# Twenty-four modulation columns of layer 0 computed as VectorE sums during the first mixer's output products, not as TensorE products during its projections

## The chip, the core and the metric

The kernel runs on one core of a Trainium2 chip. The metric is the time of one execution in microseconds (us). Three runs of the kernel before gave 1593.99, 1595.84 and 1599.15, so the median is 1595.84 us; the profiled execution, from which all durations below come, took 1600.35 us.

## What is computed

The reference is a trunk of two layers on a sequence of 512 tokens with 1024 features, all in float32. A conditioning vector `c` sets six vectors of 1024 numbers for each layer (shift, scale and gate of two sub-layers); these are the modulation:

```python
c_act = jax.nn.silu(c)
for l in range(DEPTH):                                   # DEPTH = 2
    mod = c_act @ w_ada[l] + b_ada[l]                    # 1024 x 6144
    sh_mix, sc_mix, gt_mix, sh_mlp, sc_mlp, gt_mlp = split(mod, 6)
    h = rms_norm(x, g_pre_mix[l]) * (1 + sc_mix) + sh_mix
    y = mixer(h, ...)       # w_in; 4 mLSTM heads; 8 groups of a causal depthwise conv (31 taps); w_out
    x = x + gt_mix * rms_norm(y, g_post_mix[l])
    h = rms_norm(x, g_pre_mlp[l]) * (1 + sc_mlp) + sh_mlp
    f = square(relu(h @ w_ff1[l])) @ w_ff2[l]
    x = x + gt_mlp * rms_norm(f, g_post_mlp[l])
```

## The kernel before

Features lie on the 128 partitions, so `x` is 8 tiles of 128x512, and the modulation of a layer is 48 columns of 128 numbers: columns 0 to 7 and 8 to 15 are shift and scale of the first norm, 16 to 23 the gate of the mixer, 24 to 39 shift and scale of the second norm, 40 to 47 the gate of the MLP.

A weight block of 128x1024 is loaded by SyncE's queue into one of four buffers `raw`, split by ScalarE into a rounded part (`whi`, L189) and by GpSimd into the rest (`wlo`, L190); the activations are split into such pairs too. Each product is then three passes on TensorE (L197 to L199). A `gemm` with one block is 24 passes of 128x512.

The mixer runs a list of steps (`ORDERS`, L66) by letter and number. `X` and `V` make the input and the short conv of an mLSTM head, `Q` its q, k, v and (L604) its part of the gate sums, `E` the gates from them (L614, L615), `G` one of the conv group's inputs, `Z` an output gate. `C` is the 31-tap conv of two groups on VectorE, 31 steps of 128x512 each (L450), with the group norm behind it (`conv_norm`: transposes L500 and L515 on TensorE, statistics L506 and L507, last product L521). `a` makes the weights of a head (products L683, on VectorE L675 and L685), `b` its output and norm (products L695, statistics L701 and L702, a power on GpSimd L165, scaling L715), `c` transposes it back (L724) and gates it (L726). `O` is one product with the conv half of `w_out`, whose eight input pairs are split by ScalarE and GpSimd (L173, L174). `finish` (L381) then runs the mLSTM half of `w_out`, adds (L397), and does the norms; it is the first to read columns 16 to 39.

The modulation is computed in two ways. `ada_rows` (L252) makes four columns on TensorE: four loads of 512 KB, eight products of 32x512 (L265), a copy on ScalarE (L268), four turning products (L270), and up to four small VectorE operations (L276, L278). `ada_col` (L282) makes one column on VectorE: one load of 512 KB into one of three buffers `adr`, and a product with the broadcast `c` that is summed along the row (L292, an instruction on 128x1024 and one that reads the sum out). Before the change, columns 0 to 15 of layer 0 are made ahead of the mixer by both ways, columns 16 to 39 by the six steps N4 to N9 of the first mixer's list, and the other 56 columns by `ada_col` in the first MLP. A new sum is put behind the instruction that `last[0]` names.

The program is written in this order, but a scheduler sets the order in which each engine issues; each engine then runs its instructions in that order, and a waiting instruction holds up all behind it. SyncE's queue is such an engine too: a load that waits for its buffer holds up the loads behind it.

Of the kernel before, what the change touches and what calls it, by code (L numbers as in the profile page):

```python
# [53 lines left out]
def trunk(ctx, tc, xT, vecs, bg, cst, ccol, crow, wadn, wadt, win, win0, wqkv, wgate, wout, wff1, wff2, yT):  # L54
    nc = tc.nc
    pe, dve, act, pool, sp = nc.tensor, nc.vector, nc.scalar, nc.gpsimd, nc.sync
# [6 lines left out]
    ps = ctx.enter_context(tc.tile_pool(name="ps", bufs=1, space=PSUM))  # L63

    NSLOT = 25
    ORDERS = ['X0 G3 V0 X1 Q0 V1 N4 G4 X2 G5 N5 Q1 V2 X3 N6 Q2 V3 G6 Q3 E G7 N7 Z0 Z1 Z2 Z3 N8 a0 Z4 b0 Z5 a1 b1 Z6 N9 c0 C0 a2 Z7 c1 b2 C1 C2 C3 O0 O1 a3 O2 c2 O6 O3 b3 O4 O5 c3 O7', 'X0 V0 G3 X1 Q0 V1 X2 G4 Q1 V2 G5 X3 Q2 V3 G7 Q3 E Z0 G6 Z1 Z2 Z3 a0 Z4 Z5 b0 a1 Z6 b1 Z7 c0 a2 c1 C0 b2 C1 C2 C3 O0 O1 a3 O6 O2 c2 O3 b3 O4 O5 c3 O7']  # L66
    WPRI = 300
    NK = 4
    KM = 4
# [182 lines left out]
    def ada_rows(nb, tag, alloc=None):  # L252


        bk = bank(tag)
        for kk in range(NF // 2):
            if alloc is not None:
                raw = alloc().rearrange("p a b -> p (a b)")
            else:
                raw = wpool.tile([P, D], F32, name="adr", tag="adr", bufs=ADR)  # L260
            load(raw, wadn[nb, kk])
            for j in range(2):
                k = 2 * kk + j
                g = k % 4
                pe.matmul(bk[32 * g:32 * g + 32, :], cc[:, k:k + 1].broadcast_to([P, 32]), raw[:, j * T:(j + 1) * T],  # L265
                          start=(k < 4), stop=(k >= 4), skip_group_check=True)
        rows = s2()
        act.copy(out=rows, in_=bk)  # L268
        for j in range(4):
            pe.matmul(bk[:, j:j + 1], rows[:, j * P:(j + 1) * P], cs[:, C_SEL:C_SEL + 1], start=True, stop=True)  # L270
        parts = [(2 * nb, 0, 2), (8 + 2 * nb, 2, 2)] if nb < 4 else [(4 * nb, 0, 4)]
        for c, o, n in parts:
            gain = ADA[c // 8][1]
            m, src = mods[0][:, c:c + n], bk[:, o:o + n]
            if gain is not None:
                dve.tensor_tensor(m, src, vec(gain, 0)[:, c % 8:c % 8 + n], op=ALU.mult)  # L276
                src = m
            dve.tensor_tensor(m, src, inits[0][:, c:c + n], op=ALU.add)  # L278

    late, last = [], [None]  # L280
# [155 lines left out]
    def mixer(l, hp, pre):  # L436
# [58 lines left out]
        def conv_norm(i, acc):  # L495
            csb = scr.tile([P, T], F32, name="csb", tag="csb", bufs=2)
            act.copy(out=csb, in_=acc)
            tp = bank("cx", (P, NC, P))
            for c in range(NC):
                pe.transpose(tp[:, c, :], csb[:, c * P:(c + 1) * P], ident)  # L500
            st = small(NC * 6, tag="cst6", bufs=2)
            mv = small(NC * 2, tag="cst2", bufs=2)
            stv = st.rearrange("p (c k) -> p c k", k=6)
            mvv = mv.rearrange("p (c k) -> p c k", k=2)
            for c in range(NC):
                dve.bn_stats(out=stv[:, c, :], in_=tp[:, c, :])  # L506
                dve.bn_aggr(out=mvv[:, c, :], in_=stv[:, c, :])  # L507
            r = rsqrt(mvv[:, :, 1], NC, "cm", eps=4.0 * EPS)
            ct = scr.tile([P, NC, P], F32, name="csb", tag="csb", bufs=2)
            for c in range(NC):  # L510
                dve.tensor_scalar(ct[:, c, :], tp[:, c, :], mvv[:, c, 0:1], r[:, c:c + 1],
                                  op0=ALU.subtract, op1=ALU.mult)
            bk = bank("cx")
            for c in range(NC):
                pe.transpose(bk[:, c * P:(c + 1) * P], ct[:, c, :], ident)  # L515
            th = scr.tile([P, T], F32, name="cth", tag="csb", bufs=2)
            act.activation(out=th, in_=bk, func=AF.Tanh, scale=hgb[:, l, i:i + 1], bias=hgb[:, l, 8 + i:9 + i])
            yv = cav(i)
            act.activation(out=bk, in_=bk, func=AF.Identity, scale=vec("g_cn", l)[:, i:i + 1],
                           bias=vec("b_cn", l)[:, i:i + 1])  # L520
            dve.scalar_tensor_tensor(yv, th, 1.0, bk, op0=ALU.add, op1=ALU.mult)  # L521

        def cav(i):
            if i // 2 not in caf:
# [220 lines left out]

        at[0], at[1], at[2] = glu_start(3)
        spare[0] = YM
        hm = []
        for step in ORDERS[l].split():
            i = int(step[1:] or 0)  # L750
            if step[0] == "X":
                do_xm(i)
            elif step[0] == "V":
                do_xc(i)
            elif step[0] == "G":
                at[i] = glu(i)
            elif step[0] == "Q":
                do_qkv(i)
            elif step[0] == "Z":
                z_proj(i)  # L760
            elif step[0] == "a":
                head_a(i, *g)
            elif step[0] == "b":
                head_b(i, *g)
            elif step[0] == "c":
                hm += head_c(i)
            elif step[0] == "C":
                accs = conv31([2 * i, 2 * i + 1])
                with tc.high_priority(offset=4000):
                    conv_norm(2 * i, accs[0])  # L770
                    conv_norm(2 * i + 1, accs[1])
                if i == 3:
                    ca = [conv_split(j) for j in range(NF)]
                    ypair = [slot() for _ in range(NF // 2)]
                    y = [ypair[j // 2][:, j % 2, :] for j in range(NF)]
            elif step[0] == "O":
                o = gemm([wout[l, 1, i]], ca)
                act.copy(out=y[i], in_=o)
            elif step[0] == "N":
                ada_rows(i, "ax")  # L780
            else:
                g = gates()
        return finish(l, "mix", [wout[l, 0, m] for m in range(NF)], hm, y, [ytile] * 2 + [slot] * KM,
                      ([wff1[l, m] for m in range(NK)], [slot] * NK))

# [99 lines left out]
def _layout(inp):  # L885
    f = lambda n: np.asarray(inp[n])
    col = lambda a: a.reshape(L, -1, P).transpose(2, 0, 1)
    parts = []
    for name, w in VEC_SPECS:
        a = f(name)  # L890
        if name in ("w_conv_m", "w_dw"):
            k = a.shape[1]
            parts.append(a.reshape(L, k, NF, P).transpose(3, 0, 2, 1).reshape(P, L, NF * k))
        else:
            parts.append(col(a))
    vecs = np.concatenate(parts, axis=2)
    wg = f("w_gates").reshape(L, 3, 2, P, H, 2 * H)
    wg = wg.transpose(0, 3, 4, 1, 2, 5).reshape(L, P, 24, 2 * H)
    gate = np.zeros((L, P, 24, 32), np.float32)
    gate[..., :2 * H] = wg  # L900
    kmaj = lambda a, nk, nm: a.reshape(L, nk, P, nm, P).transpose(0, 3, 2, 1, 4)
    qkv = np.stack([f("w_q"), f("w_k"), f("w_v")], axis=2)
    wo = f("w_out").reshape(L, 2, 8, P, NF, P).transpose(0, 1, 4, 3, 2, 5)
    w2 = f("w_ff2").reshape(L, 2, 2, 8, P, NF, P).transpose(0, 1, 5, 2, 4, 3, 6)
    first = [c for j in range(4) for c in (2 * j, 2 * j + 1, 8 + 2 * j, 9 + 2 * j)] + list(range(16, 40))
    return {
        "xT": f("x")[0].T.reshape(NF, P, T),
        "vecs": vecs,
        "bg": f("b_gates").reshape(L, 2, H).transpose(2, 0, 1).reshape(H, 2 * L),
        "cst": const_array(),  # L910
        "ccol": f("c").reshape(NF, P).T,
        "crow": f("c").reshape(1, D),
        "wadn": f("w_ada")[0].reshape(D, 48, P)[:, first].reshape(4, 2, P, 10, T).transpose(3, 0, 2, 1, 4).reshape(10, 4, P, D),
        "wadt": f("w_ada").transpose(0, 2, 1).reshape(L, 48, P, D),
        "win": kmaj(f("w_in"), 8, 32).reshape(L, 32, P, 1024),
        "win0": kmaj(f("w_in"), 8, 32)[0, [24, 16, 25, 17, 26, 18]].reshape(6, P, 8, P).transpose(2, 1, 0, 3).reshape(NF, P, 6 * P),
        "wqkv": qkv.reshape(L, H, 3, 2, P, DH).transpose(0, 1, 2, 4, 3, 5).reshape(L, H, 3, P, 512),
        "wgate": gate,
        "wout": wo.reshape(L, 2, NF, P, 1024),
        "wff1": kmaj(f("w_ff1"), 8, 32).reshape(L, 32, P, 1024),  # L920
        "wff2": w2.reshape(L, 2, NF, 2, P, 1024),
    }
# [18 lines left out]
```

## Time and profile before

| What | Value |
|---|---|
| Median of three runs | 1595.84 us |
| Profiled execution, span within it | 1600.35 us, 1598.6 us |
| TensorE matmuls | 1541.6 us, 96% of the span |
| VectorE | 876.3 us, 55% |
| ScalarE, GpSimd | 690.3 us (43%), 799.3 us (50%) |
| DMA | 35.4% of the engines' time, 118 GB/s |
| Mean granted TensorE clock | 0.986 |

The shares are means over the span. The first mixer, on which the change bears, ends its list at about 401 us, where `finish` begins. In the timeline an entry gives its start and its length; several equal instructions in a row are one entry with a count, and a bracket gives the idle time before it and what ended that.

### The profile page before, as it was taken

The numbers are of one execution on the slowest core, as the hardware profiler recorded it, in microseconds if no ns is written. First come the engines' busy times: TensorE is split into PE (matmuls) and PEld (weight loads), VectorE is DVE, ScalarE is ACT, GpSimd is POOL, SyncE is SP. The second block draws the span as 40 slices with busy tenths as digits, with TensorE's granted clock in tenths as the row PEclk, the third lists the DMA queues.
The fourth block names the chain that finished last, engine by engine and source line by source line (L and its number), as shares of the span: only waits on it lengthen the run. The fifth ranks groups of instructions, "written<-read, shape, count | busy, mean of one in ns | idle before, by whom it ended". The sixth has DMA issues, their size and how long they took to land.

```text
span 1598.6 us, 21226 instructions
## 1 busy us (share of the span) xinstructions
PE 1541.6 (96%) x8020; PEld 1258.7 (79%) x8020; DVE 876.3 (55%) x1761; ACT 690.3 (43%) x1168; POOL 799.3 (50%) x488
## 2 busy tenths in 40 slices
PE   5999999999999999999999999999999999999997
PEld 4776756678998888888899777676799888888887
DVE  6799998742363521347667999997226320012114
ACT  3364653444554322332463656545355432233242
POOL 0275743256744444445772877426564444444462
PEclk9999999999999999999999999998999999999999
DMA  8524323303423555556630222220241233223241
GB/s 318 188 80 147 130 96 127 137 27 106 135 64 119 185 198 180 191 192 237 214 113 1 80 74 89 82 67 27 93 146 53 85 101 93 92 92 94 97 126 54
DMA packets 56270, 188.91 MB, mean 118 GB/s; under 512 B 6376, under 2 KB 8552, under 8 KB 56168
## 3 DMA queue, kind: packets, MB, share of 16 engines
q1 hardware_dynamic: 56168, 187.56, 35.4%
q8 instruction: 63, 1.03, 0.3%
q14 instruction: 39, 0.32, 0.1%
HBM read 185.44 MB, written 2.10 MB: 117 GB/s over the span
## 4 chain that ended last, share of the span: by engine, by line
PE 78%; DVE 3%; ACT 2%; POOL 1%; issue 0%; DMA 0%; POOLq 0%; ACTq 0%
PE ps_mm L197 23%; PE ps_mm L199 23%; PE ps_mm L198 23%; PE ps_mm L695 2%; PE ps_mm L683 2%; PE ps_ax L337 1%; POOL wlo L190 1%; ACT whi L189 1%; PE ps_ax L265 1%; PE ps_ax L670 0%; PE ps_ax L599 0%; PE ps_ax L363 0%; DVE ps_cv L450 0%; PE ps_ax L724 0%; PE ps_cx L500 0%
## 5 line engine op out<-in xcount | busy, mean ns | idle before, releaser
L190 POOL TENSOR_TENSOR wlo<-raw,whi 128x1024 fp32r<-128x1024 f32 (+1 forms) x216 | 498.5, 2309 | 541.7 <-ACT whi L189 522.2
L197 PE MATMUL ps_mm<-slot,whi 128*128 128x512 f32 (+1 forms) x1632 | 621.8, 382 | 6.8 <-ACT slot L173 3.4
L199 PE MATMUL ps_mm<-slot,wlo 128*128 128x512 f32 (+1 forms) x1632 | 622.7, 382 | 4.7 <-POOL wlo L190 4.7
L198 PE MATMUL ps_mm<-slot,whi 128*128 128x512 f32 (+1 forms) x1632 | 621.2, 381 | 0.0
L189 ACT CAST whi<-raw 128x1024 fp32r<-128x1024 f32 (+1 forms) x216 | 216.4, 1002 | 509.9 <-PE ps_mm L198 369.7
L197 PEld LDWEIGHTS ps_mm<-slot,whi 128*128 128x128 f32 x1632 | 307.5, 188 | 74.8 <-issue 4.4
L199 PEld LDWEIGHTS ps_mm<-slot,wlo 128*128 128x128 f32 x1632 | 307.6, 188 | 71.3 <-POOL wlo L190 7.1
L198 PEld LDWEIGHTS ps_mm<-slot,whi 128*128 128x128 f32 x1632 | 307.6, 188 | 67.3 <-issue 5.5
L450 DVE SCALAR_TENSOR_TENSOR ps_cv<-slot,vv,ps_cv 128x512 f32<-128x512 f32 x480 | 332.6, 748 | 1.5
L790 DVE TENSOR_TENSOR ps_mm<-rl,ps_mm 128x512 f32<-128x512 f32 (+1 forms) x78 | 46.8, 600 | 282.5 <-ACT rl L789 282.4
L197 PE MATMUL ps_mm<-slot 128*128 128x256 f32 (+1 forms) x568 | 159.7, 293 | 9.6 <-DVE slot L792 7.4
L198 PE MATMUL ps_mm<-slot 128*128 128x256 f32 (+1 forms) x568 | 163.3, 292 | 0.2
L199 PE MATMUL ps_mm<-slot 128*128 128x256 f32 (+1 forms) x568 | 161.8, 289 | 0.0
L197 PEld LDWEIGHTS ps_mm<-slot 128*128 128x128 f32 x568 | 106.6, 192 | 13.0 <-DVE slot L792 8.2
L198 PEld LDWEIGHTS ps_mm<-slot 128*128 128x128 f32 x568 | 109.0, 192 | 3.2 <-issue 0.8
L199 PEld LDWEIGHTS ps_mm<-slot 128*128 128x128 f32 x568 | 108.8, 192 | 1.3
L190 POOL TENSOR_TENSOR slot<-raw,slot 128x1024 fp32r<-128x1024 f32 x34 | 86.4, 2563 | 12.8 <-issue 11.2
L165 POOL TENSOR_TENSOR small<-small,mhalf 128x4 f32<-128x4 f32 (+1 forms) x38 | 34.2, 900 | 95.5 <-DVE small L164 90.7
L292 DVE CUSTOM_DVE_ANT_0 adr<-adr,cbc,ini 128x1024 f32<-128x1024 f32 x40 | 65.4, 1645 | 23.2 <-DMA adr<-in_wadt 23.1
L792 DVE TENSOR_TENSOR slot<-ps_mm,slot 128x512 fp32r<-128x512 f32 (+1 forms) x78 | 46.4, 595 | 38.2 <-ACT slot L791 38.0
L551 POOL TENSOR_TENSOR xa<-xa,s 128x512 f32<-128x512 f32 x48 | 62.0, 1291 | 5.1 <-ACT xa L546 1.8
L791 ACT CAST slot<-ps_mm 128x512 fp32r<-128x512 f32 (+1 forms) x78 | 39.9, 511 | 46.0 <-DVE ps_mm L790 46.0
(204 smaller groups left out, 1577.3 us busy)
## 6 DMA issues: line engine op xcount, KB each, us to landing
raw<-in_wff SPq DMA_DIRECT2D x138, 512.0 KB, 3.5
raw<-in_win SPq DMA_DIRECT2D x58, 512.0 KB, 3.3
adr<-in_wadt SPq DMA_DIRECT2D x56, 512.0 KB, 4.5
raw<-in_wout SPq DMA_DIRECT2D x36, 512.0 KB, 3.5
adr<-in_wadn SPq DMA_DIRECT2D x28, 512.0 KB, 4.1
raw<-in_wqkv SPq DMA_DIRECT2D x24, 256.0 KB, 2.6
slot<-in_wadt SPq DMA_DIRECT2D x8, 512.0 KB, 8.6
raw<-in_win SPq DMA_DIRECT2D x8, 384.0 KB, 7.2
```

The costliest lines, as they stand in the source:

```text
L165: pool.tensor_tensor(y, u, mhalf[:, 0:n], op=ALU.pow)
L189: act.copy(out=r32(hi), in_=raw)
L190: wlast[0] = (lo_eng or pool).tensor_tensor(r32(lo), raw, hi, op=ALU.subtract)
L197: pe.matmul(out, whi, xh, start=first, stop=False)
L198: pe.matmul(out, whi, xl, start=False, stop=False)
L199: mark[0] = pe.matmul(out, wlo, xh, start=False, stop=last)
L292: red = dve.tensor_tensor_reduce(raw, raw, cbc, scale, 0.0 if one else ini, ALU.mult, ALU.add, m)
L450: dve.scalar_tensor_tensor(acc, at[i][:, k:k + T], w, acc, op0=ALU.mult, op1=ALU.add)
L551: pool.tensor_tensor(acc, acc, tk, op=ALU.add)
L790: dve.tensor_tensor(o, rl[:, ts], o, op=ALU.mult)
L791: act.copy(out=r32(pr[:, 0, ts]), in_=o)
L792: last[0] = dve.tensor_tensor(r32(pr[:, 1, ts]), o, pr[:, 0, ts], op=ALU.subtract)
```

## The change

The steps N4 to N9 leave the first mixer's list. In their place, from step C3 on, two `ada_col` calls follow each step until the columns 16 to 39 are done, and `ada_bias` adds the bias of the scales behind the list. `conv_norm` now names its last product (L521) in `last[0]`, so that no sum goes ahead of the latest group norm that is written before it. The `wadn` array loses the six blocks that N4 to N9 read.

```diff
-    ORDERS = ['X0 G3 V0 X1 Q0 V1 N4 G4 X2 G5 N5 Q1 V2 X3 N6 Q2 V3 G6 Q3 E G7 N7 Z0 Z1 Z2 Z3 N8 a0 Z4 b0 Z5 a1 b1 Z6 N9 c0 C0 a2 Z7 c1 b2 C1 C2 C3 O0 O1 a3 O2 c2 O6 O3 b3 O4 O5 c3 O7', ...
+    ORDERS = ['X0 G3 V0 X1 Q0 V1 G4 X2 G5 Q1 V2 X3 Q2 V3 G6 Q3 E G7 Z0 Z1 Z2 Z3 a0 Z4 b0 Z5 a1 b1 Z6 c0 C0 a2 Z7 c1 b2 C1 C2 C3 O0 O1 a3 O2 c2 O6 O3 b3 O4 O5 c3 O7', ...
@@ conv_norm
-            dve.scalar_tensor_tensor(yv, th, 1.0, bk, op0=ALU.add, op1=ALU.mult)
+            last[0] = dve.scalar_tensor_tensor(yv, th, 1.0, bk, op0=ALU.add, op1=ALU.mult)
@@ mixer
-        hm = []
+        hm, ahead = [], []
...
-            elif step[0] == "N":
-                ada_rows(i, "ax")
             else:
                 g = gates()
+            if l == 0 and step == "C3":
+                ahead = [(0, c) for c in range(16, 40)]
+            for _ in range(2):
+                if ahead:
+                    ada_col(*ahead.pop(0))
+        ada_bias()
```

Three places of the issue order show what the scheduler makes of it. Line numbers in the changed kernel are lower by one from L268 on. The first place is VectorE at the end of the last group norm. Before, head 1's statistics (L701, L702) and gating (L726) follow the norm's last product; in the changed order sums (L291, with `adr`) follow it, and between them stand operations that make head 2's weights (L684 and L674, the L685 and L675 of before; `s2` is such a weight tile). Before, behind the last L521:

```order
L521 SCALAR_TENSOR_TENSOR yt_2904<-cth_2938,ps_cx_2933 128x512
L701 BN_STATS small_2159<-slot_2140 128x6 x2
L702 BN_AGGR small_2160<-small_2159 128x2 x2
L701 BN_STATS small_2159<-slot_2140 128x6
L702 BN_AGGR small_2160<-small_2159 128x2
L726 TENSOR_TENSOR s2_2261<-ps_ax_2256,slot_1826 128x512
```

and now (the instruction that reads a sum out is left out behind each):

```order
L520 SCALAR_TENSOR_TENSOR yt_2756<-cth_2790,ps_cx_2785 128x512
L291 ISA adr_2822,mod0_101<-adr_2822,cbc_76,ini0_103,vv_74 128x1024
...
L291 ISA adr_2825,mod0_101<-adr_2825,cbc_76,ini0_103,vv_74 128x1024
...
L291 ISA adr_2860,mod0_101<-adr_2860,cbc_76,ini0_103,vv_74 128x1024
...
L684 SCALAR_TENSOR_TENSOR s2_2255<-ps_mm_2261,s2_2255 128x512
L674 SCALAR_TENSOR_TENSOR s2_2265<-ps_ax_2253,cols_1617,cs_73 128x128
L291 ISA adr_2863,mod0_101<-adr_2863,cbc_76,ini0_103,vv_74 128x1024
...
L291 ISA adr_2898,mod0_101<-adr_2898,cbc_76,ini0_103,vv_74 128x1024
```

The head's operations now stand behind and between sums; the first three sums have their data, and the fourth needs a buffer that the first frees.

The second place is VectorE at the end of head 2's norm (step b2), whose scaling (L714, before L715) TensorE's transposes of step c2 read; L712 (before L713) needs the power that GpSimd computes from L164's result. Before:

```order
L164 TENSOR_SCALAR small_2528<-small_2524 128x4
L675 SCALAR_TENSOR_TENSOR s2_3063<-ps_ax_3034,cols_1691,cs_73 128x128
L685 SCALAR_TENSOR_TENSOR s2_3036<-ps_mm_3042,s2_3036 128x512
L713 TENSOR_TENSOR small_2531<-small_2527,small_2522 128x4
L715 TENSOR_SCALAR slot_2490<-slot_2490,small_2510,small_2531 128x256 x4
```

and now:

```order
L164 TENSOR_SCALAR small_2380<-small_2376 128x4
L291 ISA adr_3209,mod0_101<-adr_3209,cbc_76,vv_74 128x1024
...
L291 ISA adr_3212,mod0_101<-adr_3212,cbc_76,vv_74 128x1024
...
L712 TENSOR_TENSOR small_2383<-small_2379,small_2374 128x4
L684 SCALAR_TENSOR_TENSOR s2_2916<-ps_mm_2921,s2_2916 128x384
L714 TENSOR_SCALAR slot_2342<-slot_2342,small_2362,small_2383 128x256 x4
L291 ISA adr_3235,mod0_101<-adr_3235,cbc_76,vv_74 128x1024
```

`adr_3212` holds the 22nd of the 24 sums, so 22 sums now stand ahead of the scaling.

The third place is SyncE's queue, where `raw_3049` holds the weights of step O3 and `raw_3140` those of O4:

```order
L127 DMA raw_3049<-in_wout 128x1024
L127 DMA adr_2863<-in_wadt 128x1024
L127 DMA adr_2898<-in_wadt 128x1024
L127 DMA adr_2901<-in_wadt 128x1024
...
L127 DMA adr_3042<-in_wadt 128x1024
L127 DMA adr_3045<-in_wadt 128x1024
L127 DMA raw_3140<-in_wout 128x1024
L127 DMA adr_3080<-in_wadt 128x1024
```

Eleven loads for sums, each of which waits for a buffer, stand between the two weight blocks; before, these two followed one another without a load between them.

## Rows read from the trace of the kernel before

**Rows 1.** The page: busy time of each engine, and of its 40 slices of 40 us VectorE's busy tenths and the granted TensorE clock in tenths.

```profile
PE 1541.6 (96%) x8020; PEld 1258.7 (79%) x8020; DVE 876.3 (55%) x1761; ACT 690.3 (43%) x1168; POOL 799.3 (50%) x488
DVE  6799998742363521347667999997226320012114
PEclk9999999999999999999999999998999999999999
```

**Rows 2.** Busy time by stretches of 40 us in the first mixer. Columns: the stretch, its length, then busy us and instructions of PE, PEld, DVE, ACT, POOL, granted clock, DMA share, GB/s.

```profile
120.00:160.00 40.00, 40.00 (x194) 27.11 (x193) 38.53 (x70) 16.04 (x25) 22.92 (x19) 1.00 0.44 148
160.00:200.00 40.00, 40.00 (x197) 28.51 (x196) 37.63 (x72) 27.66 (x47) 30.62 (x25) 1.00 0.38 129
200.00:240.00 40.00, 36.82 (x160) 23.31 (x159) 38.44 (x72) 22.11 (x37) 19.80 (x17) 0.91 0.29 95
240.00:280.00 40.00, 36.48 (x169) 25.51 (x168) 35.44 (x83) 13.98 (x19) 13.03 (x7) 0.96 0.37 129
280.00:320.00 40.00, 40.00 (x185) 25.84 (x183) 30.34 (x83) 19.41 (x43) 10.08 (x6) 1.00 0.36 135
```

**Rows 3.** TensorE's products of N4 to N9: the groups of the stretch 120 to 330 us (busy us, mean ns), and two entries of the timeline.

```profile
L265 PE MATMUL ps_ax<-adr,cc 128*32 128x512 f32 x96 | 19.6, 646 | 0.0
L270 PE MATMUL ps_ax<-cs,s 128*128 128x1 f32 x48 | 6.0, 242 | 0.0
...
140.32 1.06 PE L265 MATMUL ps_ax<-adr,cc 128*32 128x512 f32 x8
141.32 1.05 PE L270 MATMUL ps_ax<-cs,s 128*128 128x1 f32 x8
```

**Rows 4.** VectorE's timeline: 24 steps of the conv, the last head's gate sum, the last step of the conv, the last product of the last group norm, and the first addition of `finish`.

```profile
69.71 15.89 DVE L450 SCALAR_TENSOR_TENSOR ps_cv<-slot,vv,ps_cv 128x512 f32<-128x512 f32 x24
229.91 0.69 DVE L604 TENSOR_TENSOR gsb<-gsb,ps_ax 128x512 f32<-128x512 f32 x1 [0.56 <-PE ps_ax L599]
300.34 0.74 DVE L450 SCALAR_TENSOR_TENSOR ps_cv<-slot,vv,ps_cv 128x512 f32<-128x512 f32 x1
317.75 0.68 DVE L521 SCALAR_TENSOR_TENSOR yt<-cth,ps_cx 128x512 f32<-128x512 f32 x1
403.92 0.42 DVE L397 TENSOR_TENSOR slot<-slot,ps_mm 128x256 f32<-128x256 f32 x1 [7.57 <-PE ps_mm L199]
```

**Rows 5.** TensorE's timeline: the gates' first product, the last transposes of the last group norm, the transposes of step c2 and the products of head 3 behind them.

```profile
230.66 1.87 PE L614 MATMUL ps_mm<-gsb,cs 128*4 128x512 f32 x2 [0.78 <-DVE gsb L604]
315.06 0.60 PE L515 MATMUL ps_cx<-cs,csb 128*128 128x128 f32 x4
360.02 1.04 PE L724 MATMUL ps_ax<-cs,slot 128*128 128x128 f32 x8
360.89 1.47 PE L683 MATMUL ps_mm<-slot 128*128 128x256 f32 x8
```

**Rows 6.** VectorE's other operations of the stretch 80 to 345 us that step a, b and c use, by group (busy us, mean ns, idle before).

```profile
L685 DVE SCALAR_TENSOR_TENSOR s<-ps_mm,s 128x512 f32<-128x512 f32 (+3 forms) x12 | 5.8, 488 | 7.1 <-PE ps_mm L683 5.5 <-ACT s L679 1.3 <-ACT s L677 0.4
L675 DVE SCALAR_TENSOR_TENSOR s<-ps_ax,cols,cs 128x128 f32<-128x128 f32 x13 | 4.5, 347 | 5.0 <-PE ps_mm L695 3.3 <-ACT s L679 1.5 <-PE ps_ax L670 0.2
L701 DVE BATCH_NORM_STATS2 small<-slot 128x6 f32<-128x256 f32 x9 | 3.8, 425 | 1.9 <-ACT slot L697 1.8
L715 DVE TENSOR_SCALAR slot<-slot,small 128x256 f32<-128x256 f32 x8 | 2.9, 400 | 0.0
L726 DVE TENSOR_TENSOR s<-ps_ax,slot 128x512 f32<-128x512 f32 x4 | 2.8, 689 | 5.5 <-PE ps_ax L724 4.3 <-PE ps_mm L695 1.1
```

**Rows 7.** VectorE's timeline: sums of the first MLP (two that follow one another, the reading out of the second, and one later), and the same small operation of a head's norm at two times.

```profile
734.15 1.28 DVE L292 CUSTOM_DVE_ANT_0 adr<-adr,cbc,vv 128x1024 f32<-128x1024 f32 x1
735.35 3.43 DVE L292 CUSTOM_DVE_ANT_0 adr<-adr,cbc,vv 128x1024 f32<-128x1024 f32 x1
738.71 0.08 DVE L292 DVE_READ_ACCUMULATOR2_ANT mod<- 128x1 f32 x1
759.27 3.41 DVE L292 CUSTOM_DVE_ANT_0 adr<-adr,cbc,ini 128x1024 f32<-128x1024 f32 x1
...
325.57 0.16 DVE L710 TENSOR_TENSOR small<-small 128x4 f32<-128x4 f32 x1
351.05 1.19 DVE L710 TENSOR_TENSOR small<-small 128x4 f32<-128x4 f32 x1
```

**Rows 8.** GpSimd's timeline at the same times: weight splits, and the eight splits of the conv half.

```profile
734.48 3.22 POOL L190 TENSOR_TENSOR wlo<-raw,whi 128x1024 fp32r<-128x1024 f32 x1 [3.16 <-ACT whi L189]
755.85 2.40 POOL L190 TENSOR_TENSOR slot<-raw,slot 128x1024 fp32r<-128x1024 f32 x1 [1.35 <-ACT slot L189]
758.22 3.39 POOL L190 TENSOR_TENSOR wlo<-raw,whi 128x1024 fp32r<-128x1024 f32 x1
343.50 9.99 POOL L174 TENSOR_TENSOR slot<-yt,slot 128x512 fp32r<-128x512 f32 x8
```

**Rows 9.** The loads into `adr` in the stretch 730 to 785 us, where sums and weight loads follow one another fastest: from issue to landing.

```profile
DMA to landing us min/median/max: 3.2/3.8/5.2
```

**Rows 10.** Three stretches about an idle time of TensorE, with the columns of rows 2.

```profile
100.00:104.00 4.00, 1.74 (x8) 1.07 (x6) 4.00 (x7) 3.16 (x6) 3.07 (x3) 1.00 0.12 49
106.00:108.00 2.00, 2.00 (x6) 1.52 (x6) 2.00 (x4) 0.91 (x2) 2.00 (x3) 0.50 0.00 0
110.00:112.00 2.00, 2.00 (x7) 1.55 (x6) 2.00 (x4) 1.67 (x4) 1.68 (x2) 0.69 0.00 0
```

More of the change, by code (lines that the diff above doesn't have):

```diff
@@ L65, in trunk @@
     NSLOT = 25
-    ORDERS = ['X0 G3 V0 X1 Q0 V1 N4 G4 X2 G5 N5 Q1 V2 X3 N6 Q2 V3 G6 Q3 E G7 N7 Z0 Z1 Z2 Z3 N8 a0 Z4 b0 Z5 a1 b1 Z6 N9 c0 C0 a2 Z7 c1 b2 C1 C2 C3 O0 O1 a3 O2 c2 O6 O3 b3 O4 O5 c3 O7', 'X0 V0 G3 X1 Q0 V1 X2 G4 Q1 V2 G5 X3 Q2 V3 G7 Q3 E Z0 G6 Z1 Z2 Z3 a0 Z4 Z5 b0 a1 Z6 b1 Z7 c0 a2 c1 C0 b2 C1 C2 C3 O0 O1 a3 O6 O2 c2 O3 b3 O4 O5 c3 O7']
+    ORDERS = ['X0 G3 V0 X1 Q0 V1 G4 X2 G5 Q1 V2 X3 Q2 V3 G6 Q3 E G7 Z0 Z1 Z2 Z3 a0 Z4 b0 Z5 a1 b1 Z6 c0 C0 a2 Z7 c1 b2 C1 C2 C3 O0 O1 a3 O2 c2 O6 O3 b3 O4 O5 c3 O7', 'X0 V0 G3 X1 Q0 V1 X2 G4 Q1 V2 G5 X3 Q2 V3 G7 Q3 E Z0 G6 Z1 Z2 Z3 a0 Z4 Z5 b0 a1 Z6 b1 Z7 c0 a2 c1 C0 b2 C1 C2 C3 O0 O1 a3 O6 O2 c2 O3 b3 O4 O5 c3 O7']
     WPRI = 300
@@ L270, in ada_rows @@
             pe.matmul(bk[:, j:j + 1], rows[:, j * P:(j + 1) * P], cs[:, C_SEL:C_SEL + 1], start=True, stop=True)
-        parts = [(2 * nb, 0, 2), (8 + 2 * nb, 2, 2)] if nb < 4 else [(4 * nb, 0, 4)]
-        for c, o, n in parts:
+        for c, o, n in [(2 * nb, 0, 2), (8 + 2 * nb, 2, 2)]:
             gain = ADA[c // 8][1]
@@ L904, in _layout @@
     w2 = f("w_ff2").reshape(L, 2, 2, 8, P, NF, P).transpose(0, 1, 5, 2, 4, 3, 6)
-    first = [c for j in range(4) for c in (2 * j, 2 * j + 1, 8 + 2 * j, 9 + 2 * j)] + list(range(16, 40))
+    first = [c for j in range(4) for c in (2 * j, 2 * j + 1, 8 + 2 * j, 9 + 2 * j)]
     return {
@@ L912, in _layout @@
         "crow": f("c").reshape(1, D),
-        "wadn": f("w_ada")[0].reshape(D, 48, P)[:, first].reshape(4, 2, P, 10, T).transpose(3, 0, 2, 1, 4).reshape(10, 4, P, D),
+        "wadn": f("w_ada")[0].reshape(D, 48, P)[:, first].reshape(4, 2, P, 4, T).transpose(3, 0, 2, 1, 4).reshape(4, 4, P, D),
         "wadt": f("w_ada").transpose(0, 2, 1).reshape(L, 48, P, D),
```

## The prediction

> **What bounds the kernel now.** I read the page first, then the stretches of the first mixer, then timelines, for which engine's wait ends last in each stage. By the page TensorE works 96% of the span [rows 1], so any product taken from it looks like time won. But these products lie in one stage, and there the page's slices show VectorE at nine tenths. The stretches say it more sharply: from 120 to 280 us VectorE works 38.53, 37.63, 38.44 and 35.44 of each 40 us, idle 10 of 160, while TensorE has some idle time (36.82, 36.48) [rows 2]. So VectorE sets the pace up to the end of the conv at about 301 us [rows 4]; TensorE's products of the modulation are partly fill. From there to `finish` TensorE is full and VectorE's digits fall. I therefore ask when two things happen: when the last group norm's transposes run (T7, 315.06 before [rows 5]), and when TensorE gets through step c2's transposes (360.02 [rows 5]) to `finish`, whose first addition stands at 403.92 [rows 4]. Behind that the order of all engines is practically the same in both kernels, so the shift there is the shift of the end.
>
> **What is removed.** N4 to N9 hold 96 products (19.6 us busy) and 48 turning records (6.0) [rows 3]. Ends overlap: a group of eight takes about 1.05, so 12 + 6 groups are 18 to 19 us by starts, and 25.6 by busy time; with the waits on the copy between I take 24. The ten small VectorE operations and six ScalarE copies are little (about 1.4 us on VectorE before the last conv step). The 24 loads become 24 others of the same 512 KB; I cost them at nothing, since DMA is at 0.29 to 0.44 there [rows 2].
>
> **Step 1, the gates.** Head 4's gate sum stands at 229.91 and TensorE waits 0.78 for it [rows 4, 5]. In the changed order four conv steps of 0.66 (24 take 15.89 [rows 4]) and one L521 (0.68) stand behind it instead of ahead, and five modulation operations (0.8) are gone: 4.1 earlier, and 1.3 more as VectorE waits less for TensorE: 224.5. TensorE, without N4 to N6 (half of 24), would be there 12 earlier, at 218.7, so it waits 6 there: half of this gain goes.
>
> **Step 2, to the last conv step.** Before, 71.2 us lie from the gate sum's start to that step's end (300.34 + 0.74). Now the work of step 1 that moved behind and parts of heads 1 and 2 (three L675, four L685, statistics) come on top, by the durations in [rows 4, 6] about 7.3 net of removed operations. Some 7.5 of the 71.2 were idle; I take 5 of it back. 71.2 + 7.3 - 5 = 73.5, so the step ends at 298, not 301.
>
> **Step 3, T7.** From there to T7 were 14.0; with N9's turns out I take 13: T7 = 311. Bounds: 315 if the 14 us of TensorE work that now stand ahead of T7 (c0's transposes, Z6, a2's products) fill what was freed, 306 if step 2's idle goes altogether and step 1 loses nothing.
>
> **Step 4, VectorE from the last L521 to b2's scaling.** This is the step that decides. L521 ends 3.4 behind T7 (317.75 + 0.68 - 315.06 [rows 4, 5]). In the changed order 22 sums stand between it and b2's scaling, and step c2's transposes read what that scaling writes. TensorE runs in order, so c2 holds O2 and all behind. Its terms:
> - 22 sums of 1.28 and 0.08 for reading out [rows 7]: 29.9.
> - The others there: seven operations of a2, six of a3, two L726, four L701 with L702, about six small, four L715: by the means in [rows 6] about 11.
> - Waiting for data. With three buffers a sum can come every (3.8 + 1.36) / 3 = 1.72 us at the median landing and 2.19 at the longest [rows 9], against 1.86 of VectorE work per sum (40.9 / 22). Bounds 0 and 22 x 0.33 less what contention hides, at most 6.3; I take 2.
> - Contention with GpSimd. A sum beside a GpSimd split takes 3.43 and 3.41 instead of 1.28 [rows 7], and the split 3.22 and 3.39 instead of 2.40 [rows 8]. So the pair takes 3.4 where one after the other would take 3.68: only 0.28 is gained by overlap. Even a small operation went from 0.16 to 1.19 during the conv half's splits [rows 7, 8]. GpSimd has 17.3 us in this stretch: eight such splits (9.99 [rows 8]), two of the same length for the heads (2.5) and two weight splits (4.8). At 3.4 - 1.28 = 2.1 per 2.4, that is 15.5 at most, 0 if the splits fall beside other work or ahead; I take 10, nearer to the upper row, as the sums leave VectorE hardly a gap.
>
> 29.9 + 11 + 2 + 10 = 53, bounds 41 and 62.
>
> The Trainium skill has a rule that speaks against this change ("SBUF — State Buffer", section "Who interferes with whom"): a VectorE instruction with two SBUF inputs and a GpSimd instruction that reads SBUF shut each other out for whole instructions. By it each split would cost its full length, 17.3 for 15.5 at the upper end; the trace nearly agrees, 3.4 for the pair against 3.68.
>
> **Step 5, c2 to `finish`.** 403.92 - 360.02 = 43.9 before. Head 3's eight L683 (1.47 [rows 5]) now stand ahead of c2: 42.5. But TensorE's own work from T7 to c2 is only about 31 now (45 before less the 14 of step 3), against 56.4 of VectorE's chain, so it stands still for some 25 us. After an idle 2.26 of 4 us, about 102 us, the granted clock was 0.50 in one stretch and 0.69 in another some us later [rows 10]; so the first products behind a wait of 25 us may go at half speed too: 0 to 3 us, I take 1.7, about what those two stretches lost together (1.0 and 0.62 us).
>
> **Sum.** 311 + 3.4 + 53 + 42.5 + 1.7 = 411.6 for the first addition of `finish`, 7.7 later than 403.92. The profiled execution took 1600.35 us, 4.5 above the median of 1595.84; 1600.35 + 7.7 = 1608.1 stands to the median as 1604. The stretch of step 4 at which nothing changes is 53 - 7.7 = 45.
>
> **Rivals.**
> - **No change.** The stretch is 40.5 to 50 us, or T7 comes early: half of the contention taken (5 for 10) and no wait for data gives 46, and +1 us. For it: the eight splits of the conv half may run mainly before the first sums, since ScalarE writes their other half early. Against it: they stood at 343.50, 25 us behind the last L521 [rows 4, 8]. 1591 to 1601, middle 1596.
> - **The other side: VectorE hides the sums.** One mechanism: GpSimd's splits don't meet the sums, so that step 4 costs its own 41 us, and T7 comes early, at 306. Then c2 starts 17 earlier than in my forecast, without the wait that slows the clock, and `finish` at 306 + 3.4 + 41 + 42.5 = 392.9, 11 earlier: 1585. It decides from a stretch below 40.5 at T7 = 311, or 45 at 306. For it: VectorE has slack behind 320 us (30.34 of 40 in 280 to 320 [rows 2], four and two tenths of the slices after [rows 1]), and sums in the first MLP do run at 1.28 [rows 7]. The face value of the change, all 24 us, at 1572, is the far end of this; the bound of VectorE before 280 us speaks against it.
> - **SyncE's queue.** Eleven loads for sums stand ahead of O4's weight block. Each waits for a buffer, so that block is issued when the eleventh sum behind is through, about 28 us behind T7, and is split about 7 later; TensorE comes to O4 some 75 behind T7 (56.4 to c2, then O2, O6 and O3). It costs nothing unless sums are 40 us late; then those 40 would come on top of a kernel already slower, 1620 or more. It falls within slower.
> - **The change doesn't do what it says**: sums go elsewhere. The issue order shows them behind the last L521, so I give it nothing.
>
> **How the numbers follow.** A difference under 0.3%, 4.8 us, is about what a measurement of this kernel can't tell from none. Forecast, slower than that: the stretch is over 50 us, as three of its four terms have prices in the rows: 0.58, with 0.03 of SyncE's queue in it. No change: 0.26. The other side: 0.16, of which 0.03 for the face value. At the ends, 306 with 41 gives -11, 315 with 62 gives +22; both at once are unlikely, so the range is 1588 to 1614 (-8 and +18), which leaves out about one in ten on either side.
>
> **What would show it right or wrong.** Right: the last L521 at about 314.4; TensorE waiting some 6 us for the gate sum; sums of 2.3 to 3.4 us where GpSimd splits beside them and 1.28 elsewhere; b2's scaling done at about 367; an idle time of TensorE of 20 us or more ahead of c2's transposes, released by VectorE's scaling; a lower granted clock behind; the first addition of `finish` at about 411.6 and everything behind it as before. Wrong: c2 starts before 360, T7 before 306, or TensorE waits for a weight block of O4 or O5 rather than for VectorE.

## The result

The changed kernel takes 1615.42 us (median of four, 1614.96 to 1616.51) against 1597.49 of the kernel before (four runs beside it): slower, ratio 1.0117, 95% interval 1.0103 to 1.0131. The forecast was 1604, with a range up to 1614. The sign was right, and so was the mechanism in the first mixer. The loss is twice the forecast, mainly because as much again comes behind that mixer, where nothing was forecast.

The profiled execution took 1614.96 us. Against the profiled one of before that is 14.6 more: 7.5 up to the first addition of `finish` (411.46 against 403.92 [rows 4]; forecast 411.6) and 7.1 behind it (forecast 0). The rest of the 17.9 is that the profiled execution of before lay 2.9 above the median of its four runs, that of the changed kernel 0.5 below its own.

### The profile page after: what moved, and what is told of

It is laid out like the page before. It is cut to its first block, busy times and chain, and to the rows that moved or that the text cites. A ratio compares the mean times of both kernels' runs of the same rounds, so it can differ in the third digit from the quotient of the medians.

```text
span 1613.2 us, 20970 instructions
## 1 busy us (share of the span) xinstructions
PE 1527.5 (95%) x7876; PEld 1257.8 (78%) x7876; DVE 911.8 (57%) x1800; ACT 685.8 (43%) x1162; POOL 805.5 (50%) x488
## 4 chain that ended last, share of the span: by engine, by line
PE 79%; DVE 5%; DMA 2%; ACT 2%; POOL 1%; issue 1%; SPq 0%; POOLq 0%; ACTq 0%; DVEq 0%
PE ps_mm L197 24%; PE ps_mm L198 24%; PE ps_mm L199 24%; PE ps_mm L694 2%; PE ps_mm L682 2%; DMA adr<-in_wadt 2%; DVE adr L291 1%; DVE ps_cv L449 1%; PE ps_ax L336 1%; POOL wlo L190 1%; PE ps_ax L598 1%; ACT whi L189 1%; PE ps_ax L669 0%; PE ps_ax L362 0%; PE ps_ax L723 0%
## 5 line engine op out<-in xcount | busy, mean ns | idle before, releaser
L291 DVE CUSTOM_DVE_ANT_0 adr<-adr,cbc,ini 128x1024 f32<-128x1024 f32 x56 | 87.8, 1577 | 27.0 <-DMA adr<-in_wadt 26.9
L291 DVE CUSTOM_DVE_ANT_0 adr<-adr,cbc,vv 128x1024 f32<-128x1024 f32 x24 | 41.9, 1764 | 34.2 <-DMA adr<-in_wadt 34.0
```

The lines of the kernel that those rows point to most:

```text
L291: red = dve.tensor_tensor_reduce(raw, raw, cbc, scale, 0.0 if one else ini, ALU.mult, ALU.add, m)
```

## The profile after

The page, as in [rows 1]: TensorE works 14 us less, VectorE 35 more, and VectorE's ninth slice (320 to 360 us) has gone from 4 to 9.

```profile
PE 1527.5 (95%) x7876; PEld 1257.8 (78%) x7876; DVE 911.8 (57%) x1800; ACT 685.8 (43%) x1162; POOL 805.5 (50%) x488
DVE  6799998893254422347556999996326320012114
PEclk9999999988999999999999999998999999999999
```

The stretches of [rows 2] and the two behind them (start and end, length, busy us of PE, PEld, DVE, ACT, POOL, granted clock, DMA share, GB/s):

```profile
160.00:200.00 40.00, 39.22 (x186) 28.62 (x185) 39.00 (x75) 25.50 (x42) 33.24 (x28) 1.00 0.24 75
200.00:240.00 40.00, 30.75 (x129) 20.86 (x129) 39.88 (x69) 18.33 (x27) 15.18 (x12) 0.96 0.26 83
320.00:360.00 40.00, 31.95 (x110) 22.45 (x110) 36.65 (x61) 15.24 (x34) 23.27 (x13) 0.87 0.71 236
360.00:400.00 40.00, 34.49 (x144) 28.36 (x145) 16.84 (x36) 10.26 (x16) 22.77 (x11) 0.87 0.43 149
```

From 200 to 240 us TensorE is busy 30.75 of 40, where it was 36.82, while VectorE is busy 39.88: TensorE has fewer products to fill its waits. From 320 to 360 us VectorE is the bound (36.65 of 40), and TensorE idles and has a lower clock (0.87).

VectorE's timeline at the points of [rows 4]: gate sum, last conv step, last product of the last group norm, two sums and the small operation L712 beside splits, head 2's scaling, first addition of `finish`. Then the two splits on GpSimd.

```profile
222.40 0.67 DVE L603 TENSOR_TENSOR gsb<-gsb,ps_ax 128x512 f32<-128x512 f32 x1
296.15 0.75 DVE L449 SCALAR_TENSOR_TENSOR ps_cv<-slot,vv,ps_cv 128x512 f32<-128x512 f32 x1
312.02 0.69 DVE L520 SCALAR_TENSOR_TENSOR yt<-cth,ps_cx 128x512 f32<-128x512 f32 x1
358.20 1.28 DVE L291 CUSTOM_DVE_ANT_0 adr<-adr,cbc,vv 128x1024 f32<-128x1024 f32 x1 [0.77 <-DMA adr<-in_wadt]
359.64 3.13 DVE L291 CUSTOM_DVE_ANT_0 adr<-adr,cbc,vv 128x1024 f32<-128x1024 f32 x1
362.70 2.28 DVE L712 TENSOR_TENSOR small<-small 128x4 f32<-128x4 f32 x1
365.38 1.37 DVE L714 TENSOR_SCALAR slot<-slot,small 128x256 f32<-128x256 f32 x4
411.46 0.42 DVE L396 TENSOR_TENSOR slot<-slot,ps_mm 128x256 f32<-128x256 f32 x1 [7.58 <-PE ps_mm L199]
...
358.49 3.20 POOL L190 TENSOR_TENSOR wlo<-raw,whi 128x1024 fp32r<-128x1024 f32 x1
361.65 3.31 POOL L190 TENSOR_TENSOR wlo<-raw,whi 128x1024 fp32r<-128x1024 f32 x1
```

TensorE's timeline at the points of [rows 5]: the gates' product, the last norm's transposes (309.93; forecast 311), then its longer waits, and c2's transposes (366.52). Three of the four are for VectorE's L684 (head 2's and 3's weights), one is for ScalarE; none is for the scaling itself:

```profile
223.13 1.02 PE L613 MATMUL ps_mm<-gsb,cs 128*4 128x512 f32 x2 [1.91 <-DVE gsb L603]
309.93 0.60 PE L514 MATMUL ps_cx<-cs,csb 128*128 128x128 f32 x4
317.17 1.23 PE L682 MATMUL ps_mm<-slot 128*128 128x128 f32 x4 [4.09 <-DVE s L684]
321.91 0.80 PE L197 MATMUL ps_mm<-slot,whi 128*128 128x512 f32 x1 [3.52 <-DVE s L684]
336.36 2.93 PE L694 MATMUL ps_mm<-slot,s 128*128 128x257 f32 x8 [1.99 <-ACT slot L696]
365.51 1.22 PE L682 MATMUL ps_mm<-slot 128*128 128x128 f32 x4 [6.41 <-DVE s L684]
366.52 0.64 PE L723 MATMUL ps_ax<-cs,slot 128*128 128x128 f32 x2
```

Behind the first addition of `finish`, TensorE waits longer or at places where the kernel before does not: for VectorE at the first MLP's start (1.11, where it was 0.44), a second time for a weight split at that MLP's end, and for the splits of the conv half in the second layer's mixer:

```profile
490.09 0.39 PE L197 MATMUL ps_mm<-slot 128*128 128x256 f32 x1 [1.11 <-DVE slot L795]
772.93 0.50 PE L199 MATMUL ps_mm<-slot,wlo 128*128 128x512 f32 x1 [1.54 <-POOL wlo L190]
782.94 0.50 PE L199 MATMUL ps_mm<-slot,wlo 128*128 128x512 f32 x1 [2.14 <-POOL wlo L190]
1128.06 0.73 PE L197 MATMUL ps_mm<-slot,whi 128*128 128x512 f32 x2 [0.68 <-ACT slot L173]
1129.41 0.50 PE L198 MATMUL ps_mm<-slot,whi 128*128 128x512 f32 x1 [0.63 <-POOL slot L174]
```

The kernel before has one wait for a weight split there:

```profile
771.65 0.51 PE L199 MATMUL ps_mm<-slot,wlo 128*128 128x512 f32 x1 [2.08 <-POOL wlo L190]
```

## The experiments

All ratios are to runs of the kernel before on the same chip, with 95% intervals. Where lines of an edit are left out, the text says so.

### Two more traces of the same kernels

No edit.

> The kernel before, unchanged, for a second trace of it. In the first traces of the two kernels the changed one reaches the first addition of finish 7.5 us later (411.46 against 403.92), but ends 14.6 us later: 7 us come behind it, where both issue the same instructions in the same order (1194.7 us from that addition to the end of the span before, 1201.7 after). Theory A: these 7 us are the state of one execution (which sums of the first MLP meet which weight splits), so a second trace of the same kernel gives another value, spread over several us, between 1190 and 1200. Theory B: they belong to the change, so this trace gives 1194.7 within 1 us.

> The changed kernel, unchanged, for a second trace. First addition of finish at 411.5 within 1 us by both theories. From there to the end: theory A, another value than 1201.7, as likely near 1195; theory B, 1201.7 within 1 us. Time against before: +17 to +18 us as measured (ratio about 1.0117).

Measured: before 1.0011 (0.9997 to 1.0025); changed 1.0109 (1.0092 to 1.0125). From the first addition to the end it took 1191.8 and 1198.7 us, where the first traces had 1194.7 and 1201.7. So each kernel varies by 3 us, and 7 us lie between them both times: neither theory holds alone. A large part of what varies is the clock. An estimate of what it costs is the sum of 2 x (1 - granted clock) over slices of 2 us. By it TensorE loses 1.7 us at a time, behind a wait, and the same wait has this in one execution and not in another. The second split wait of the changed kernel has it in the first trace,

```profile
784.00:786.00 2.00, 2.00 (x7) 1.61 (x6) 0.00 (x0) 1.41 (x2) 2.00 (x1) 0.61 0.70 252
786.00:788.00 2.00, 2.00 (x6) 1.53 (x6) 0.00 (x0) 1.21 (x2) 2.00 (x2) 0.54 0.36 66
```

and not in the second:

```profile
784.00:786.00 2.00, 2.00 (x10) 1.58 (x10) 0.00 (x0) 1.25 (x2) 2.00 (x2) 1.00 0.54 209
```

The table has ten traces, eight of them of this and of later experiments: from the first addition of `finish` to the gates of the second layer (L614), to the first addition of that layer's `finish`, and to the end. Times are in us; brackets have what the clock took by that sum, without the last 40 us, where every kernel loses about 3.

| Kernel | first addition | to gates | to finish | to end | total less clock |
|---|---|---|---|---|---|
| before | 403.9 | 604.2 (1.7) | 162.7 (5.1) | 427.8 (1.7) | 1186.2 |
| e1_before_again | 403.2 | 604.0 (1.7) | 160.0 (3.4) | 427.8 (1.7) | 1185.0 |
| changed | 411.5 | 611.0 (5.1) | 165.1 (5.1) | 425.6 (0) | 1191.5 |
| e1_after_again | 410.8 | 609.6 (3.4) | 163.6 (3.4) | 425.5 (0) | 1191.9 |
| e1_none | 387.7 | 608.4 (3.4) | 163.7 (6.8) | 428.3 (1.7) | 1188.5 |
| e1_behind_b2 | 403.0 | 604.9 (1.7) | 160.1 (3.4) | 428.3 (1.7) | 1186.4 |
| e2_after_w10 | 410.4 | 609.5 (3.4) | 165.2 (5.1) | 425.5 (0) | 1191.7 |
| e3_pin | 409.1 | 609.4 (3.4) | 165.4 (8.5) | 425.6 (0) | 1188.5 |
| e3_after_smooth | 413.9 | 606.0 (5.1) | 162.4 (3.4) | 425.3 (0) | 1185.1 |
| e3_before_smooth | 400.5 | 601.9 (1.7) | 160.3 (3.4) | 427.7 (1.7) | 1183.1 |

Less the clock, three traces of the changed kernel (e2_after_w10 is that kernel with a larger input array) agree within 0.4 us and two of before within 1.2. Between their means lie 6.1 us, and that part belongs to the change. Between the first two traces of the changed kernel the clock accounts for the whole difference of 3.0 us, between those of before only for 1.7 of 2.9; what made the rest is not known.

### No sums at all

```diff
-                ahead = [(0, c) for c in range(16, 40)]
+                dve.tensor_copy(out=mods[0][:, 16:40], in_=inits[0][:, 16:40])
```

> The changed kernel with no sums in the first mixer: columns 16 to 39 of layer 0 are only the biases, so the modulation of those columns is left out. It shows what TensorE's removed products are worth alone, 24 us at most. Theory (VectorE sets the pace to the last conv step): the last group norm's transposes at about 310, as in the changed kernel, step c2's transposes about 31 later at 341 to 343, first addition of finish at 384 to 387, 17 to 20 us earlier than before. Rival 1, TensorE is the bound: all 24 us, finish at 380. Rival 2, VectorE's chain of the conv and the heads binds to the end: finish at 395 or later.

Measured: 0.9941 (0.9924 to 0.9957). The last norm's transposes come at 311.41, c2's at 343.36 and c3's at 378.19, the first addition at 387.70:

```profile
343.36 1.03 PE L723 MATMUL ps_ax<-cs,slot 128*128 128x128 f32 x8
378.19 1.03 PE L723 MATMUL ps_ax<-cs,slot 128*128 128x128 f32 x8
```

So the removed products are worth 16 us at `finish` of the 24 that the prediction gave them, a little below what was expected, and both rivals fall. That VectorE ahead of the norm keeps the rest fits the rows, but is not tested by itself. In the time of the whole kernel 9 us are won: sums that cost nothing would have won no more than that here. Behind `finish` this kernel has the issue order of before on every engine and yet takes 1188.5 less clock, 2.9 more than before: the same order is not the same time.

### The sums behind head 2's scaling

```diff
                 ahead = [(0, c) for c in range(16, 40)]
+                last[0] = scaled[2]
```

`scaled[2]` is the last L714 of head 2; the two lines that keep it are left out.

> The changed kernel with one thing moved: no sum goes ahead of the scaling of head 2's norm (step b2). By the issue order the sums then run beside O2 to O7 and the first product of finish, and SyncE's loads for them alternate with weight blocks. Theory (the loss is the 22 sums ahead of that scaling): step c2's transposes at 341 to 345 instead of 366.5, first addition of finish at 386 to 392 after some waits for weight splits that the sums slow, 12 to 18 us earlier than before. Rival 1, contention with GpSimd and the loads take the gain back: weight splits are late for O4 to O7, finish at 400 to 412. Rival 2, the loss does not lie in that place of the order: finish at 411 as in the changed kernel.

Measured: 1.0029 (1.0012 to 1.0047), first addition at 403.00. c2's transposes come at 344.41 as the theory has it, so the place of the sums held them. But the gain is gone by `finish`. Rival 1 had this time (400 to 412), but not the place, which no theory named: 16 sums now stand ahead of head 3's scaling, and the last ones, stretched to 3.4 us beside weight splits, ahead of the first addition:

```profile
344.41 1.03 PE L723 MATMUL ps_ax<-cs,slot 128*128 128x128 f32 x8
383.66 2.27 PE L723 MATMUL ps_ax<-cs,slot 128*128 128x128 f32 x8 [4.03 <-DVE slot L714]
403.46 0.39 PE L197 MATMUL ps_mm<-slot 128*128 128x256 f32 x1 [2.13 <-DVE slot L396]
```

c3's transposes take 2.27 us here and 1.03 in e1_none: behind the wait TensorE runs at the lower clock (granted 0.50 from 382 to 388 us).

### Half the sums, in the same place

```diff
-                ahead = [(0, c) for c in range(16, 40)]
+                ahead = [(0, c) for c in range(16, 28)]
+                dve.tensor_copy(out=mods[0][:, 28:40], in_=inits[0][:, 28:40])
```

> The changed kernel with the first 12 of its 24 sums, in the same place; columns 28 to 39 of layer 0 are only the biases. By the issue order all 12 stand ahead of head 2's scaling where 22 stood. Theory (those sums hold c2): VectorE's stretch from the last group norm to the scaling falls from 54 us by ten sums of 1.36 and their contention to 32 to 38, so step c2's transposes at 345 to 351 instead of 366.5, and the first addition of finish at 388 to 394. Rival (what holds c2 is not the number of sums, but SyncE's loads or GpSimd): c2 at 358 or later, finish at 402 or later.

Measured: 1.0028 (1.0011 to 1.0044). The scaling is done at 349.95, 37.75 us behind the norm's last product, c2 starts at 353.32, and the first addition comes at 397.32, some 2 to 3 us later than expected and far from the rival:

```profile
348.57 1.38 DVE L714 TENSOR_SCALAR slot<-slot,small 128x256 f32<-128x256 f32 x4
353.32 1.04 PE L723 MATMUL ps_ax<-cs,slot 128*128 128x128 f32 x8
```

From 12 to 22 sums the stretch grows by 16.3 us, 1.6 a sum. With 12 sums the scaling is done before TensorE comes to c2 and no longer holds it; what is left of the delay are waits of 4.09, 3.60 and 1.89 us, two for weights of the heads and one for ScalarE.

### The size of the input array

```diff
-    first = [c for j in range(4) for c in (2 * j, 2 * j + 1, 8 + 2 * j, 9 + 2 * j)]
+    first = [c for j in range(4) for c in (2 * j, 2 * j + 1, 8 + 2 * j, 9 + 2 * j)] + list(range(16, 40))
```

The line that shapes `wadn` to ten blocks is left out.

> As e1_none (no sums in the first mixer, columns 16 to 39 of layer 0 are only the biases), but the array of row blocks keeps the ten blocks it had before, six of them unread, so that no input has another size than in the kernel before. Behind finish its issue order on every engine is that of the kernel before, yet e1_none took 1200.4 us from the first addition of finish to the end where the kernel before took 1194.7 and 1191.8. Theory P (the six blocks less move the other inputs in memory, and that shifts their loads): 1191 to 1196 here. Theory T (the earlier or later arrival in the first MLP and its own loads decide, whatever the sizes): 1199 to 1201 again.

> The changed kernel, and nothing else than that array at its old size. Theory P: TensorE's second wait in the first MLP (2.14 us for a weight split at 782.94, then a lower clock) is gone and the time falls by 3 to 6 us, to a ratio of about 1.008. Theory T: as the changed kernel, ratio 1.011, with that second wait.

Measured: 0.9937 (0.9922 to 0.9952) and 1.0114 (1.0094 to 1.0135); the second wait for a split stays in both (2.18 and 2.15 us). So theory P falls. e2_none_w10 does take 1195.0 us to the end, as P had it, but 1189.9 less clock, no less than e1_none (1188.5).

### The order in the second mixer put back

```diff
+                        if l and j == 6:
+                            behind(tanhs[l, 7], hi_inst[0])
+                            behind(copies[l, 2, 2], hi_inst[0])
```

The lines that keep these three instructions are left out.

> The changed kernel with one piece of order put back: in the second layer's mixer ScalarE makes seven casts of the conv half ahead of the last group norm's tanh and of head 2's third copy, as in the kernel before; the changed kernel has them behind. Theory A1 (of the 7 us behind finish, a part is issue order that the scheduler chose anew there): TensorE's waits of 0.68 and 0.63 us for those casts and their splits, at 1128 in the changed kernel, are gone, and from the gates of the second layer to the first addition of its finish it takes 160.0 to 163.7 us, where the three traces of the changed kernel show 163.6 to 165.2; the time falls by 1 to 3 us. Rival (the order there costs nothing, executions differ): 163.6 to 165.2 again.

Measured: 1.0118 (1.0103 to 1.0134), and 165.4 us between gates and `finish`. The two waits are gone, and less the clock the stretch falls from 160.1 to 156.9 us, that of before (156.6 and 157.6). But the clock takes 8.5 us instead of 5.1 or 3.4, and the time shows no gain. So the order explains 3 us of the trace; that putting it back saves time is not shown.

### The first MLP's sums spread

```diff
-                some(1)
+                some(1 + hf * (m % 2))
...
                     last[0] = dve.tensor_tensor(y[m], y[m], o, op=ALU.add)
-                    some(2)
+                    some(1)
```

> The changed kernel with the sums of the first MLP spread more evenly: in its second half two per two products become three, and one instead of two behind each product of the last eight. Theory A2 (of the 7 us behind finish, a part comes from sums that stand bunched at the end of the first MLP and hold GpSimd's weight splits): TensorE's waits of 1.54 and 2.14 us for splits there are gone, from the first addition of finish to the end it takes 1193 to 1198 us instead of 1198.7 to 1201.7, ratio 1.006 to 1.009. Rival (the splits are late for their loads): the waits stay, 1199 to 1202.

> The kernel before with the same spreading of the first MLP's sums. Theory A2: its one wait of 1.9 to 2.1 us for a split at 771 is gone, ratio 0.997 to 0.999; so less falls here than in the changed kernel. Rival: 1.000.

Measured: changed kernel 1.0064 (1.0037 to 1.0091), kernel before 0.9995 (0.9984 to 1.0005). The split waits are gone in both, so the bunched sums do make them, as A2 had it. The changed kernel gains about 5 in 1000 by it; its six runs spread from 1600.6 to 1614.5 us, so the size is uncertain. The kernel before gains nothing that can be measured, against A2's 1 to 3 in 1000. Less clock the way to the gates is 600.9 against 600.2, where the means of the table are 606.0 against 602.4: of 3.6 us more, 2.9 go with the bunched sums.

### Half by TensorE, half by sums in the free place

```diff
+... 'X0 G3 V0 X1 Q0 V1 N4 G4 X2 G5 N5 Q1 V2 X3 N6 Q2 V3 ...
+                ahead = [(0, c) for c in range(28, 40)]
+                last[0] = scaled[2]
```

The lines that bring back `ada_rows` for these steps and their part of `wadn`, and those that keep `scaled`, are left out.

> Columns 16 to 27 by TensorE in steps N4 to N6, where they were before; columns 28 to 39 by 12 sums that stand behind head 2's scaling. By the issue order they then stand ahead of head 3's statistics. Theory (VectorE sets the pace ahead of the last conv step, so N4 to N6 cost TensorE little of use, and N7 to N9 cost 12 us; 12 sums fit between the two heads' scalings): first addition of finish at 393 to 398, time 4 to 10 us below the kernel before less what comes back in the first MLP, a ratio of 0.994 to 0.999. Rival 1 (the sums meet the weight splits of O2 to O5 and hold them, or head 3's norm): finish at 400 to 406, ratio 1.000 to 1.004. Rival 2 (N4 to N6 cost as much as N7 to N9): finish at 400 even without a wait behind c2.

> e2_keep456 (columns 16 to 27 by TensorE, 28 to 39 by sums behind head 2's scaling) with the first MLP's sums spread. First addition of finish at 393 to 395 as there. Theory A2: its wait of 2.12 us at 762 is gone too and the time is 2 to 5 us below that of e2_keep456, ratio 0.9955 to 0.9975. Rival: 0.9986 again.

Measured: 0.9986 (0.9973 to 0.9999), and with the spread sums 0.9980 (0.9966 to 0.9995): both are below the kernel before, but by only 1 to 2 in 1000, hardly outside the interval. The first addition comes at 393.70 and 394.2. In the first of the two TensorE comes to c2 at 347.81 and waits 0.56 at c3 (line numbers are here as in the kernel before):

```profile
347.81 1.04 PE L724 MATMUL ps_ax<-cs,slot 128*128 128x128 f32 x8
383.56 1.71 PE L724 MATMUL ps_ax<-cs,slot 128*128 128x128 f32 x8 [0.56 <-DVE slot L715]
```

So N4 to N6 may stay, and 12 sums fit between the two scalings. Of the 9 to 10 us won at `finish` 3 are left between the medians. The trace shows a part of why: with the spread sums this kernel lost 11.9 us to the clock behind the first addition, where the two traces of before lost 8.5 and 6.8. The split wait is gone, but a gain by the spreading, expected at 2 to 5 us, is not shown: the two intervals overlap.

## Why the prediction was wrong

**The first mixer, steps 1 to 5: right.** Gate sum 222.4 (forecast 224.5), last conv step done 296.9 (298), T7 309.9 (311), last L521 ended 312.7 (314.4), stretch to head 2's scaling 54.0 (53), scaling done 366.75 (367), c2 to first addition 44.9 (44.2), first addition 411.46 (411.6). That the last figure is met within 0.2 us is luck: the misses of the terms, 1.7 early and then 1.7 late, cancel. For the gate sum itself TensorE waited 1.91 us and not 6; its waits from 200 to 224 us come to 6.3, but most are for ScalarE. Inside the stretch, 22 sums took 37.7 us, 9.6 above 1.28 each (contention taken as 10), reading out 1.8, and waits for loads 4.3 (taken as 2). The groups, with two sums that come behind the scaling:

```profile
L291 DVE CUSTOM_DVE_ANT_0 adr<-adr,cbc,ini 128x1024 f32<-128x1024 f32 x16 | 26.0, 1637 | 3.7 <-DMA adr<-in_wadt 3.5
L291 DVE CUSTOM_DVE_ANT_0 adr<-adr,cbc,vv 128x1024 f32<-128x1024 f32 x8 | 14.1, 1765 | 0.9 <-DMA adr<-in_wadt 0.8
```

**Where the wait shows: half wrong.** It was to be one idle time of 20 us or more ahead of c2, ended by the scaling. From T7 to c2 TensorE was idle for 19.2 us, but in eight pieces: 4.09, 3.52, 1.99, 6.41 and four under 1.8, mostly for heads' weights that VectorE makes between sums. From 318 to 326 us and from 364 to 370, behind the longer ones, its granted clock was 0.50. The sum came out because the whole chain was summed on VectorE.

**"Behind that the order of all engines is practically the same in both kernels, so the shift there is the shift of the end": the step that failed.** Two things were wrong in it. The first is that the orders differ, also against what the first expectations say: the scheduler had reordered small pieces at the starts of both MLPs and in the second mixer. In the second mixer ScalarE has, before and now (other instructions left out):

```
L697 COPY, L697 COPY, L173 CAST x7, L697 COPY, L517 tanh
L696 COPY, L516 tanh, L518, L696 COPY, L696 COPY, L173 CAST x7
```

So the conv half is split later and O0 waits. This is 3.0 us less clock (160.1 against 157.1).

The second is that equal order does not give equal time. To the gates of the second layer the changed kernel takes 3.6 us more less clock, of which e3_after_smooth and e3_before_smooth take away 2.9. TensorE's waits in the first MLP show where: in each of the three traces 2.6 us more than in the first of before (8.5 against 5.9), 0.9 at the MLP's start, where the order differs, and 1.6 at its end, where one wait for a split has become two. e1_none has these two with the order of before, so the order does not make the second. The time of arrival alone does not make it either: e1_behind_b2 and e1_before_again reach `finish` at 403.0 and 403.2, and the one has two waits (1.56 and 2.16), the other one (1.90). What makes one wait into two stays open.

Against these two parts the second MLP and the end have 0.5 less, and the clock adds 0.85 (8.5 on the mean of three traces against 7.7 of two). Together that makes the 7.0 us between the means.

**The base.** I took 4.5 us off the sum because the profiled execution of before lay above the median of three. But the changed kernel's profiled execution lay at its own median. So of the 11.4 us missed some 7 lie behind the first addition, and 4.5 are this subtraction, an error that has nothing to do with the change.

**The rivals.** No change and VectorE hiding the sums are both out, the latter at its own point: the stretch was 54, not below 40.5. SyncE's queue cost nothing at O4: no wait for a weight block of O4 or O5 stands among TensorE's waits.

**The rule on SBUF.** The prediction took the pair of sum and split at 3.4 us, the length of the longer of the two. But these lengths contain waiting, and the rows of 358 to 365 us show for what. The sum of 358.20 ends at 359.48. The split of 358.49 ends at 361.69, 2.2 behind that. The sum of 359.64 ends at 362.77, 1.1 behind the split. L712 then ends at 364.98, and the split of 361.65 at 364.96. So they work almost one after the other: from 359.48 on, split and sum took 3.3 us, and in [rows 7, 8] from 735.43 on 3.35. By the rule (the Trainium skill, "SBUF — State Buffer", "Who interferes with whom") it would be 2.40 + 1.28 = 3.68. The trace agrees with it but for 0.3 to 0.4 us. By it step 4 would have had up to 17.3 of contention; the 9.6 measured in the sums are near the 10 taken, since only 8 of the 22 sums were held by splits (1.95 to 3.13 us each, the others at most 1.41).

**Open.** Besides the second split wait, TensorE's pace in the MLP: 24 products take 5.553 us in both traces of before and about 5.573 in the changed kernel and in those cut from it, spread over all products. The array's size is not the cause; no run here shows what is. It is 0.36%, by an estimate some 1 us in the first MLP, and with the second wait it is about what e1_none has more than before.

## What to carry to other kernels

Work that is taken off the busiest engine must be priced on the chain of the engine that gets it, at the place where its in-order queue puts it: here 22 sums of 1.7 us stood ahead of one short scaling. Ask also what the work filled: of the 24 us of removed products only 16 were time won when nothing took their place. And a shift is carried to the end only as far as the schedule behind it is rigid: compare the orders there piece by piece, and put a spread of several us on it where bunched work on two engines holds each other up, as the sums and the splits do here.

## What the runs showed of the hardware

- A fall of TensorE's granted clock to 0.5, the lower of its two levels (1.2 of 2.4 GHz), costs 1.7 us here or a multiple of it by the sum over slices, behind a wait, in some executions and not in others. With these taken out, traces of the changed kernel agree within 0.4 us and those of before within 1.2, where the raw ones differ by 3.
- A VectorE sum and a GpSimd split, both on 128x1024, work almost one after the other (3.3 us for 2.40 and 1.28 alone), and the profile counts the one that waits as busy: the sum then shows 3.13 us, the split 3.20.
- VectorE's small operations are held too: in e1_behind_b2 L712 on 128x4 took 2.29 us at 380.77, beside a weight split of 2.33 us that began at 380.71, so both end together; at 339.68 it took 0.17.
